# The MLP of a decoder trunk: one level of Strassen's scheme in its expanding product, and eight chunks of hidden channels for four

## The chip, the cores and the metric

One core of one Trainium2 chip. Times are device microseconds of one execution, and a kernel's time is the median of its runs. TensorE (PE) multiplies, VectorE (DVE), ScalarE (ACT) and GpSimd (POOL) do the rest, SyncE (SP) starts transfers.

## The reference

Two layers on 512 tokens of 1024 channels, all float32. What matters here is the second half of a layer, with 4096 hidden channels:

```python
u = rms_norm(h, mlp_norm_w[l])
h = h + jnp.square(jax.nn.relu(u @ w_mlp_in[l])) @ w_mlp_out[l]
```

The first half (three token mixers from one input product, and an output product into the residual stream) and the final norm stay as they are.

## The kernel before

The residual stream lies channel-major in SBUF: eight tiles `h[m]` of 128 channels by 512 tokens. Every dense product is exact to nearly float32 by splitting each operand into two float32r parts, high and low. A k tile then takes three matmuls, high by high, high by low and low by high, added up in PSUM. `load_w` (L875) fetches a tile of weights, 128 x 4 x 256, as `raw`; a copy (ACT or DVE) makes its high part `whi`, and a subtraction `raw - whi` its low part `wlo`. The norm's factor for each token is applied after the expanding product (it commutes with relu): `finish_h` (L809) squares a finished `h[m]` into the sum `sqa`, and splits `h[m]` times the norm's weight into `u`; `norm_stats` makes the row of factors `rb`.

The MLP (L1102) goes through the hidden channels in 4 chunks of 1024: `expand(q)` (8 tiles of 128 channels by 512 tokens, 24 matmuls of 512 columns each, `mm_cm`), then relu times `rb`, the square, and its split into `hh` and `hl`; `contract(q)` adds the chunk's share to the eight `h[m]`. The order in the program is expand(0), expand(1), contract(0), and so on. The last chunk of the last layer contracts token-major, with 256 columns (`mm_tm`), since the final norm goes on from there.

Nothing runs in program order. A recorder takes down every operation (in the profile all have L483, pairs of attention products L1275). A list scheduler then fixes one order per engine from the costs in `cost` (matmul: columns/2.4 + 2.7 ns; GpSimd: 80 + 2.2 ns a column), with 12 rounds of forward and backward schedules, and each engine runs its list strictly in order. An operation that several engines could do (`copy`: ACT or DVE; `tt`: DVE or GpSimd) goes to its first choice unless another would be done clearly earlier. How many tiles of a kind exist is set by `CAPS` (L523): a tile's slot is reused when its last reader is done. The costs know of no influence of one engine on another.

Of the kernel before, what the change touches and what calls it, by code (L numbers as in the profile page):

```python
# [10 lines left out]
F32 = mybir.dt.float32  # L11
# [56 lines left out]
class Buf:  # L68
    """A tile, allocated when its first instruction is emitted."""
# [26 lines left out]
class View:  # L96
    """A part of a tile: the steps that lead to it, and its shape."""
# [85 lines left out]
class Recorder:  # L183
    """Records the instructions, orders them for the engines, and emits them in that order."""
# [38 lines left out]
    def add(self, eng, run, outs, ins, dur, lat=0.0):  # L223
# [9 lines left out]
        # a product's start clears its whole bank  # L233
# [17 lines left out]
    def order(self):  # L251
        """List schedules: first by the longest path, then by the start times of a backward schedule."""
# [28 lines left out]
    def backward(self, span):  # L281
        """From the end, with the tiles in the order they had: the latest starts."""
# [34 lines left out]
    def forward(self):  # L317
# [37 lines left out]
        while done < len(ops):  # L355
# [25 lines left out]
            # the tiles it allocates  # L381
# [20 lines left out]
            if op.ways:  # L402
                # the first way's engine has it unless another would be done with it clearly earlier
# [60 lines left out]
class _Engine:  # L464
# [23 lines left out]
    def cost(self, method, named, views):  # L488
# [6 lines left out]
        if self.eng == "PE":  # L495
# [8 lines left out]
            return (112.0 if m <= 64 else 214.0), 0.0  # L504
# [18 lines left out]
CAPS = {"u": 16, "un": 28, "hw": 6, "lg": 10, "pt": 4, "raw": 2, "whi": 4, "wlo": 4, "t2": 5, "mm": 3, "mx": 5, "hq": 4,  # L523
# [6 lines left out]
class Build:  # L530
# [10 lines left out]
    def tile(self, shape, dt=F32, tag=None):  # L541
        """A tile of a tag's slots; without a tag, one that stays."""
# [38 lines left out]
    # ---------------------------------------------------------------- setup  # L581
    def setup(self):
# [3 lines left out]
        # the tensor engine at its full clock before the input is there  # L586
# [10 lines left out]
        # the input, channel-major  # L597
# [210 lines left out]
    # ---------------------------------------------------------------- norms  # L808
    def finish_h(self, m, key, l, src=None):  # L809
        """h[m] is final: its squares, and its split and weighted form for the next products."""  # L810
# [4 lines left out]
        if key is not None:  # L815
# [30 lines left out]
    def row_bc(self, cols, o=None):  # L846
        """cols [128 tokens of a tile, 4 tiles] -> [128, 512], each row the 512 tokens' values."""
# [52 lines left out]
    def load_cols(self, pieces, n, per):  # L900
        """pieces: (column in the tile, DRAM AP [1024, columns]) -> split weights, per rows of 128 to a tile."""
# [14 lines left out]
    def mm_cm(self, out, w, c0, m, x, kts=range(KT)):  # L916
        """channel-major: out[m channels, 512 tokens]."""
# [9 lines left out]
    def mm_tm(self, out, t, w, n, x):  # L927
        """token-major: out[128 tokens of tile t, n columns]."""
# [8 lines left out]
    # ---------------------------------------------------------------- one layer  # L937
    def layer(self, l):
# [7 lines left out]
        # --- the indexer's queries; latent keys; the values of the sparse attention with the indexer's keys and weights  # L946
# [28 lines left out]
        # --- small weights of the layer  # L975
# [15 lines left out]
        # the second part's halves, one under the other  # L991
# [4 lines left out]
        # --- latent queries  # L996
# [23 lines left out]
        # --- gated linear recurrence, two heads at a time  # L1020
# [29 lines left out]
        # --- sparse attention  # L1050
# [30 lines left out]
        # --- output product  # L1081
# [20 lines left out]
        # --- MLP  # L1102
        self.norm_stats()
        x, rb = self.u, self.rb
        hid = [None] * 4

        def expand(q):
            tags = ["un"] * 16 if q % 2 == 0 else ["un"] * 2 + ["lg"] * 8 + ["hw"] * 6
            H = [self.tile((128, 512), F32R, t) for t in tags]
            H = (H[:8], H[8:])  # L1110
            for j in range(4):
                c = q * 1024 + j * 256
                w = self.load_w([(0, a["w_mlp_in"][l][:, c:c + 256])], 256, False)
                for i in range(2):
                    m = 2 * j + i
                    p = self.psm()
                    self.mm_cm(p, w, i * 128, 128, x)
                    r, r2 = self.t2(), self.t2()
                    hh, hl = H[0][m], H[1][m]
                    nc.vector.scalar_tensor_tensor(r, p, 0.0, rb, op0=OP.max, op1=OP.mult)  # L1120
                    nc.square(hh, r)
                    nc.tt(r2, r, r, OP.mult)
                    nc.tt(hl, r2, hh.bitcast(F32), OP.subtract)
            hid[q] = H
# [63 lines left out]
    def index_scores(self, l, qi, ki, wi):  # L1188
        """0 for the selected keys and -NEG for the others, for the query tiles that have more than N_SEL keys."""
# [45 lines left out]
                # float32r is at its full rate from 256 columns on  # L1235
# [30 lines left out]
    def pair(self, po, vals, PT, k):  # L1266
        """Two heads' products, side by side on the array."""
# [89 lines left out]
    # ---------------------------------------------------------------- gated linear recurrence  # L1357
# [12 lines left out]
    def hgrn_head(self, l, hd, hf, pq, vi, gate, cq, mix):  # L1370
# [82 lines left out]
        # the norm over the head's channels, the gate  # L1453
# [104 lines left out]
```

## Time and profile before

| | |
|---|---|
| median of three runs | 1389.15 us (1389.15 to 1390.95) |
| profiled execution: time of the runs beside it / its span | 1389.15 / 1388.4 us |
| PE busy | 1349.8 us, 97% |
| DVE, ACT, POOL busy | 903.3, 546.9, 175.3 us |
| mean granted TensorE clock over the span | 0.989 |
| moved by DMA | 131.52 MB, mean 95 GB/s |

A busy share is an average over parts of the program that differ. A wait counts if the engine that waits is the one that the end of the program hangs on; so the stretches, the chain that ended last and the idle time before single instructions are read along with it.

### The profile page before, as it was taken

How to read it: one execution, taken by the hardware profiler on the slowest of the kernel's cores; microseconds unless marked ns; L12 is line 12 of the kernel's file. 1: busy time of each engine (PE TensorE's matmuls, PEld its weight loads, DVE VectorE, ACT ScalarE, POOL GpSimd, SP SyncE). 2: the span in 40 equal slices, each digit the busy share in tenths (PEclk: the TensorE clock that was granted, in tenths of full speed). 3: DMA queues.
4: the chain of work that ended last, by engine and by line, in shares of the span. 5: the costliest groups of instructions: out<-in, count | busy, mean ns of one | idle time of the engine just before them, and what ended most of it. 6: DMA issues, size and time to landing. Idle time of an engine off the chain costs nothing.

```text
span 1388.4 us, 17965 instructions
## 1 busy us (share of the span) xinstructions
PE 1349.8 (97%) x6693; PEld 1094.5 (79%) x6693; DVE 903.3 (65%) x1863; ACT 546.9 (39%) x1002; POOL 175.3 (13%) x145
## 2 busy tenths in 40 slices
PE   8899999999999999999999999999999999999998
PEld 5688887767788878878778878877678888878897
DVE  6979999795755354354446999988586534534444
ACT  5556447364333122132234674546343312312233
POOL 3213223040100000000002213214010000000000
PEclk9999999999999999999999999999999999999999
DMA  7433121143233333232435212223332323233322
GB/s 229 119 109 88 46 77 47 53 146 124 73 101 95 93 102 96 83 99 91 136 106 120 62 31 76 76 69 102 118 92 81 113 79 106 91 91 107 104 80 76
DMA packets 137083, 131.52 MB, mean 95 GB/s; under 512 B 14068, under 2 KB 129540, under 8 KB 136996
## 3 DMA queue, kind: packets, MB, share of 16 engines
q1 hardware_dynamic: 135716, 127.62, 30.5%
q0 software_dynamic: 1280, 2.77, 0.9%
q8 instruction: 52, 0.85, 0.3%
q14 instruction: 35, 0.29, 0.1%
HBM read 121.44 MB, written 8.92 MB: 94 GB/s over the span
## 4 chain that ended last, share of the span: by engine, by line
PE 83%; DVE 12%; issue 2%; ACT 2%; DMA 1%; SPq 0%; DVEq 0%; ACTq 0%
PE mm L483 73%; PE mx L483 9%; DVE un L483 5%; DVE c L483 2%; DVE t L483 1%; DVE lg L483 1%; PE mx L1275 1%; DVE wlo L483 1%; DVE hw L483 1%; DMA raw<-in_w_in_dram 1%; ACT t L483 1%; ACT un L483 0%; DVE sqa L483 0%; DVE ge L483 0%; ACT whi L483 0%
## 5 line engine op out<-in xcount | busy, mean ns | idle before, releaser
L483 PE MATMUL mm<-u,whi 128*128 128x512 f32 x1632 | 515.0, 403 | 5.4 <-ACT whi L483 3.6
L483 ACT ACTIVATE whi<-raw 128x1024 fp32r<-128x1024 f32 (+2 forms) x198 | 205.3, 1039 | 480.7 <-PE mm L483 437.5
L483 PEld LDWEIGHTS mm<-u,whi 128*128 128x128 f32 x1632 | 305.5, 189 | 78.1 <-ACT whi L483 4.2
L483 DVE TENSOR_TENSOR wlo<-raw,whi 128x1024 fp32r<-128x1024 f32 (+1 forms) x170 | 207.9, 1225 | 219.0 <-ACT whi L483 183.8
L483 PE MATMUL mm<-u,wlo 128*128 128x512 f32 x816 | 293.9, 401 | 2.5 <-DVE wlo L483 2.5
L483 PE MATMUL mm<-un,whi 128*128 128x512 f32 x816 | 260.1, 401 | 3.2 <-DVE un L483 3.1
L483 PEld LDWEIGHTS mm<-un,whi 128*128 128x128 f32 x816 | 153.5, 189 | 41.7 <-DVE un L483 3.7
L483 PEld LDWEIGHTS mm<-u,wlo 128*128 128x128 f32 x816 | 153.2, 188 | 39.2 <-DVE wlo L483 3.3
L483 PE MATMUL mm<-un,wlo 128*128 128x512 f32 x432 | 159.4, 400 | 0.0
L483 DVE TENSOR_TENSOR un<-mm,un 128x512 f32<-128x512 f32 (+2 forms) x120 | 77.6, 652 | 118.0 <-PE mm L483 106.8
L483 PE MATMUL mm<-whi,u 128*128 128x256 f32 (+1 forms) x640 | 139.5, 304 | 0.4 <-DVE un L483 0.3
L483 POOL TENSOR_TENSOR wlo<-raw,whi 128x1024 fp32r<-128x1024 f32 (+3 forms) x38 | 92.1, 2424 | 311.6 <-ACT whi L483 204.7
L483 PE MATMUL mx<-un,un 128*128 128x512 f32 (+3 forms) x380 | 117.0, 374 | 10.0 <-DVE un L483 7.2
L483 PEld LDWEIGHTS mm<-whi,u 128*128 128x128 f32 x640 | 103.8, 192 | 10.5 <-issue 6.2
L483 PEld LDWEIGHTS mm<-un,wlo 128*128 128x128 f32 x432 | 81.7, 190 | 19.4 <-issue 0.7
L483 PEld LDWEIGHTS mx<-un,un 128*128 128x128 f32 x380 | 69.2, 195 | 25.6 <-DVE un L483 9.1
L483 DVE SCALAR_TENSOR_TENSOR t<-mm,rb 128x512 f32<-128x512 f32 x68 | 46.6, 689 | 64.7 <-PE mm L483 63.6
L483 PE MATMUL mm<-wlo,u 128*128 128x256 f32 (+1 forms) x320 | 84.9, 306 | 0.0
L483 PE MATMUL mm<-lg,whi 128*128 128x512 f32 x192 | 70.3, 395 | 0.0
L483 ACT ACTIVATE un<-t 128x512 fp32r<-128x512 f32 (+1 forms) x63 | 39.6, 630 | 64.1 <-DVE t L483 62.3
L483 PEld LDWEIGHTS mm<-wlo,u 128*128 128x128 f32 x320 | 56.8, 192 | 3.3 <-issue 2.1
L483 PE MATMUL mm<-hw,whi 128*128 128x512 f32 x144 | 54.7, 394 | 0.0
(203 smaller groups left out, 1664.6 us busy)
## 6 DMA issues: line engine op xcount, KB each, us to landing
raw<-in_w_mlp_in_dram SPq DMA_DIRECT2D x64, 512.0 KB, 3.6
raw<-in_w_mlp_out_dram SPq DMA_DIRECT2D x64, 512.0 KB, 3.5
raw<-in_w_in_dram SPq DMA_DIRECT2D x42, 512.0 KB, 3.8
d<-un SPq DMA_DIRECT2D x20, 256.0 KB, 3.2
raw<-in_w_in_dram SPq DMA_DIRECT2D x18, 256.0 KB, 3.2
raw<-in_w_out_dram SPq DMA_DIRECT2D x16, 256.0 KB, 2.7
raw<-in_w_out_dram SPq DMA_DIRECT2D x8, 512.0 KB, 3.4
un<-d SPq DMA_DIRECT2D x16, 256.0 KB, 4.9
```

Source lines behind the costliest of these rows:

```text
L483: real(*[res(v) for v in args], **{k: res(v) for k, v in kw.items()})
L1275: self.real.tensor.matmul(outs[i].get(), vals[i].get(), rhs[i].get(), start=k == 0, stop=k == NT - 1)
```

## The change

With the input x and a weight matrix of one chunk cut into quarters (by 512 channels in, and 256 tokens or 256 hidden channels), the expanding product needs eight products of quarters. The changed kernel takes seven, in the Strassen-Winograd form: products of sums and differences of quarters, whose results are added up. A chunk is now 512 hidden channels, and there are eight. The sums over x (`forms`) are made once per layer, the differences of weights in each chunk. Matmuls have 256 columns (half the tokens). The contraction stays a plain product, also cut into 256 columns. The caps and the costs of PE change with it. Comments and docstrings are gone, which says nothing.

```diff
-                return n * (1 if n >= 256 else 4) / 2.4 + 2.7, 0.0
+                return n * (0.4453 if n >= 256 else 1.7) + 4.0, 0.0
-CAPS = {"u": 16, "un": 28, ... "pt": 4, "raw": 2, "whi": 4, "wlo": 4, "t2": 5, ...
+CAPS = {"u": 16, "un": 24, ... "pt": 3, "raw": 5, "whi": 5, "wlo": 5, "t2": 6, ...
+        if key == "mn":
+            self.forms(m, self.v(key, l, m))
+    def forms(self, m, w):
...
+        f = self.un()
+        nc.copy(f, hm, w)
+        if m < 4:
+            hi, lo = self.X["X11"][k]
+            nc.copy(hi, f[:, half[0]])
+            nc.tt(lo, f[:, half[0]], hi.bitcast(F32), OP.subtract)
+            return
+        nc.copy(hi, f)
+        nc.tt(lo, f, hi.bitcast(F32), OP.subtract)
+        nc.tt(S1, x21, x22, OP.add)
+        nc.tt(S3, x11, x21, OP.subtract, True)
+        nc.tt(S2, S1, x11, OP.subtract)
+        nc.tt(S4, x12, S2, OP.subtract)
+        if k % 2:
+            for n, t in self.S.items():
+                nc.copy(hi, t)
+                nc.tt(lo, t, hi.bitcast(F32), OP.subtract)
...
+        def activate(q, c, i, b):
+            nc.vector.scalar_tensor_tensor(v(r), v(c), 0.0, tok, op0=OP.max, op1=OP.mult)
+            nc.square(hh, r)
+            nc.tt(r, r, r, OP.mult, True)
+            nc.tt(hl, r, hh.bitcast(F32), OP.subtract)
         def expand(q):
+            A, B, C = self.ps(), self.psm(), self.ps()
+            s11 = split(w11)
+            nc.tt(w11, w12, w11, OP.subtract, True)
+            product(A, "X11", s11, True, False)
+            p1 = self.t2()
+            nc.copy(p1, A)
+            product(B, "X12", split(w21), True, True)
+            nc.vector.tensor_tensor(out=p1, in0=B, in1=p1, op=OP.add)
+            activate(q, p1, 0, 0)
+            nc.tt(w12, w22, w12, OP.subtract, True)
+            s22 = split(w22)
+            nc.tt(w22, w22, w11, OP.subtract, True)
+            product(A, "S2", split(w22), False, False)
+            u = self.t2()
+            nc.copy(u, A)
+            product(C, "S1", split(w11), True, False)
+            p5 = self.t2()
+            nc.copy(p5, C)
+            product(A, "S3", split(w12), False, False)
+            nc.vector.tensor_tensor(out=p5, in0=A, in1=p5, op=OP.add)
+            activate(q, p5, 1, 1)
+            product(C, "S4", s22, False, True)
+            nc.vector.tensor_tensor(out=u, in0=C, in1=u, op=OP.add)
+            activate(q, u, 0, 1)
+            nc.tt(w21, w21, w22, OP.subtract, True)
+            product(A, "X22", split(w21), False, True)
+            activate(q, A, 1, 0)
         def contract(q):
...
+                    for i in range(2):
+                        o = p[:, i * 256:i * 256 + 256]
+                        for k in range(4):
+                            xh, xl = (x(i, k, part) for part in range(2))
+                            nc.tensor.matmul(o, wh[:, k, ms], xh, start=k == 0, stop=False)
+                            nc.tensor.matmul(o, wh[:, k, ms], xl, start=False, stop=False)
+                            nc.tensor.matmul(o, wl[:, k, ms], xh, start=False, stop=k == 3)
```

`split` makes a high and a low part of a tile of weights, `product` runs 2 x 4 x 3 matmuls into one PSUM bank, and `True` as the last argument of `nc.tt` names GpSimd as first choice. The differences of weights are written over the raw tiles in place.

What this does to the order is shown at the start of an MLP's product and in a steady chunk. First DVE in a steady chunk before (names: a kind of tile, the tile's number, the number of the operation that wrote it; out<-in); `raw`, `whi`, `wlo` are weights, `t2` and `un` hidden channels, `mm` a PSUM bank:

```order
L483 TENSOR_TENSOR wlo_1081_4137<-raw_1079_4069,whi_1080_4130 128x1024
L483 SCALAR_TENSOR_TENSOR t2_1046_4156<-mm_1045_4034,rb_993_3993 128x512
L483 TENSOR_TENSOR t2_1047_4164<-t2_1046_4156 128x512
L483 TENSOR_TENSOR un_1011_4170<-t2_1047_4164,un_1003_4162 128x512
L483 SCALAR_TENSOR_TENSOR t2_1049_4177<-mm_1048_4089,rb_993_3993 128x512
L483 TENSOR_TENSOR wlo_1084_4182<-raw_1082_4117,whi_1083_4173 128x1024
```

One subtraction of weights stands to about three operations on hidden channels. DVE in chunk 4 of layer 0 now, where `un<-mm,un` are additions into the residual stream and `raw_1219` to `raw_1222` the four quarters of weights w11, w12, w22 and w21:

```order
L483 TENSOR_TENSOR wlo_1227_5532<-raw_1219_5328,whi_1226_5455 128x1024
L483 TENSOR_TENSOR un_919_3522<-mm_1203_5451,un_919_3522 128x512
L483 TENSOR_TENSOR un_927_3678<-mm_1207_5475,un_927_3678 128x512
L483 TENSOR_TENSOR un_929_3680<-mm_1208_5490,un_929_3680 128x512
L483 TENSOR_TENSOR wlo_1230_5567<-raw_1222_5425,whi_1229_5528 128x1024
L483 TENSOR_TENSOR wlo_1234_5580<-raw_1221_5402,whi_1233_5556 128x1024
L483 SCALAR_TENSOR_TENSOR t2_1196_5593<-mx_1170_4993,rb_1021_4138 128x512
L483 TENSOR_TENSOR raw_1221_5402<-raw_1221_5402,raw_1219_5328 128x1024
L483 TENSOR_TENSOR raw_1222_5425<-raw_1222_5425,raw_1221_5402 128x1024
L483 TENSOR_TENSOR un_1198_5633<-t2_1196_5593,un_1197_5602 128x512
L483 TENSOR_TENSOR wlo_1236_5640<-raw_1221_5402,whi_1235_5622 128x1024
```

Four subtractions for splits and two of the differences of weights stand there among the additions. GpSimd beside it now:

```order
L483 TENSOR_TENSOR raw_1219_5328<-raw_1220_5356,raw_1219_5328 128x1024
L483 TENSOR_TENSOR raw_1220_5356<-raw_1221_5402,raw_1220_5356 128x1024
L483 TENSOR_TENSOR t2_1196_5593<-t2_1196_5593 128x512
L483 TENSOR_TENSOR t2_1228_5614<-t2_1228_5614 128x512
```

The other two differences and the squares are GpSimd's. On PE the last use of `wlo_1201`, whose slot `wlo_1227` takes, is the first row here, and the first uses of the difference w22 - w11' (`whi_1235`, `wlo_1236`, for the product with S2 into the bank `mx_1223`) are the third and the last; 84 and 93 matmuls lie between:

```order
L483 MATMUL mm_1203_5451<-un_1137_4945,wlo_1201_5343 128x256
...
L483 MATMUL mm_1213_5586<-un_1145_5156,whi_1210_5392 128x256
L483 MATMUL mx_1223_5469<-hw_965_3937,whi_1235_5622 128x256
L483 MATMUL mm_1212_5562<-un_1144_5125,wlo_1211_5408 128x256
...
L483 MATMUL mm_1212_5562<-un_1138_4980,whi_1210_5392 128x256
L483 MATMUL mx_1223_5469<-hw_965_3937,wlo_1236_5640 128x256
```

PE takes the matmuls of the contraction (`mm`) and of the products (`mx`) in turn. At the start of the MLP of layer 0, DVE before had additions into the residual stream, the sum of squares and the low parts `u`:

```order
L483 TENSOR_TENSOR sqa_959_3759<-sqa_959_3759,t2_987_3881 128x512
L483 SCALAR_TENSOR_TENSOR u_978_3909<-un_939_3515,k_26_151,u_977_3899 128x512
L483 SCALAR_TENSOR_TENSOR u_982_3918<-un_947_3713,k_26_151,u_981_3911 128x512
L483 SCALAR_TENSOR_TENSOR u_986_3926<-un_949_3724,k_26_151,u_985_3920 128x512
```

GpSimd had the last subtractions of `load_w` for the output product there. Now it has four differences of weights, sums over x and squares (DVE has as many sums over x beside these, and the splits):

```order
L483 TENSOR_TENSOR raw_1027_3310<-raw_1028_3574,raw_1027_3310 128x1024
L483 TENSOR_TENSOR raw_1028_3574<-raw_1029_3620,raw_1028_3574 128x1024
L483 TENSOR_TENSOR u_960_3827<-un_983_3810,u_958_3821 128x256
L483 TENSOR_TENSOR raw_1029_3620<-raw_1029_3620,raw_1027_3310 128x1024
L483 TENSOR_TENSOR un_992_3865<-un_977_3771,un_989_3851 128x256
L483 TENSOR_TENSOR raw_1030_3669<-raw_1030_3669,raw_1029_3620 128x1024
L483 TENSOR_TENSOR un_993_3900<-un_992_3865,un_977_3771 128x256
```

Of the seven rows four write over raw weights, and three make sums over x that go into the forms.

## Rows read from the trace of the kernel before

**Rows 1.** Page, part 1: busy us, share of the span, instructions by engine.

```profile
PE 1349.8 (97%) x6693; PEld 1094.5 (79%) x6693; DVE 903.3 (65%) x1863; ACT 546.9 (39%) x1002; POOL 175.3 (13%) x145
```

**Rows 2.** Stretches inside the MLPs: PE, PEld, DVE, ACT, POOL, clock, DMA share, GB/s.

```profile
380.00:520.00 140.00, 139.79 (x603) 112.84 (x602) 69.06 (x84) 37.53 (x43) 1.86 (x1) 1.00 0.31 95
1040.00:1320.00 280.00, 280.00 (x1206) 225.84 (x1206) 131.62 (x158) 70.14 (x79) 5.63 (x5) 1.00 0.32 98
```

**Rows 3.** Chain that ended last, MLP steps: start, us, engine, tile, count.

```profile
364.46 152.09 PE mm L483 x655
...
1032.79 288.27 PE mm L483 x1240
...
1343.67 29.33 PE mm L483 x248
```

**Rows 4.** Groups by form, 360 to 760: busy, mean ns; idle before, releaser.

```profile
L483 DVE TENSOR_TENSOR wlo<-raw,whi 128x1024 fp32r<-128x1024 f32 x68 | 83.2, 1223 | 118.1 <-ACT whi L483 92.0 <-PE mm L483 26.1
L483 ACT ACTIVATE whi<-raw 128x1024 fp32r<-128x1024 f32 x68 | 72.1, 1061 | 212.7 <-PE mm L483 181.6 <-DVE t L483 11.8 <-issue 10.2
L483 DVE TENSOR_TENSOR un<-mm,un 128x512 f32<-128x512 f32 x32 | 22.1, 690 | 45.6 <-PE mm L483 45.5
```

**Rows 5.** Groups by form of GpSimd, whole span.

```profile
L483 POOL TENSOR_TENSOR wlo<-raw,whi 128x1024 fp32r<-128x1024 f32 x32 | 78.0, 2436 | 268.6 <-ACT whi L483 192.3 <-PE mm L483 66.7 <-DVE whi L483 4.8
...
L483 POOL TENSOR_TENSOR sqa<-sqa,t 128x512 f32<-128x512 f32 x3 | 3.9, 1284 | 266.3 <-ACT t L483 263.6 <-ACT sqa L483 2.3 <-DVE t L483 0.5
...
L483 POOL TENSOR_TENSOR hw<-hw,c 128x256 f32<-128x256 f32 x4 | 2.6, 648 | 7.1 <-DVE hw L483 7.1
```

**Rows 6.** Timeline of GpSimd, 335 to 360: start, us, instruction, idle before.

```profile
342.87 2.41 POOL L483 TENSOR_TENSOR wlo<-raw,whi 128x1024 fp32r<-128x1024 f32 x1 [31.70 <-ACT whi L483]
349.99 2.97 POOL L483 TENSOR_TENSOR wlo<-raw,whi 128x1024 fp32r<-128x1024 f32 x1 [4.71 <-ACT whi L483]
```

**Rows 7.** Timeline of DVE, the same time.

```profile
341.77 1.22 DVE L483 TENSOR_TENSOR wlo<-raw,whi 128x1024 fp32r<-128x1024 f32 x1
342.90 0.68 DVE L483 TENSOR_TENSOR un<-mm,un 128x512 f32<-128x512 f32 x1
343.50 2.33 DVE L483 TENSOR_TENSOR sqa<-sqa,t 128x512 f32<-128x512 f32 x1
345.76 0.68 DVE L483 TENSOR_TENSOR un<-mm,un 128x512 f32<-128x512 f32 x1
...
350.02 0.68 DVE L483 TENSOR_TENSOR sqa<-sqa,t 128x512 f32<-128x512 f32 x1
350.62 2.90 DVE L483 SCALAR_TENSOR_TENSOR u<-un,k,u 128x512 fp32r<-128x512 f32 x1
```

**Rows 8.** Timeline of PE at the start of the MLP of layer 0.

```profile
346.49 1.20 PE L483 MATMUL mm<-un,whi 128*128 128x512 f32 x4 [1.21 <-DVE un L483]
...
355.43 0.44 PE L483 MATMUL mx<-k,sqa 128*128 128x64 f32 x2 [1.36 <-DVE sqa L483]
```

**Rows 9.** Stretches where PE pauses, columns as in rows 2.

```profile
350.00:360.00 10.00, 8.64 (x42) 6.82 (x41) 8.72 (x17) 4.87 (x9) 2.96 (x1) 1.00 0.18 52
970.00:975.00 5.00, 2.98 (x16) 2.20 (x15) 4.71 (x9) 1.78 (x8) 3.60 (x2) 1.00 0.86 300
975.00:980.00 5.00, 4.76 (x21) 3.01 (x22) 4.85 (x16) 2.89 (x7) 0.04 (x1) 0.66 0.36 112
```

**Rows 10.** Timeline of DVE near the end.

```profile
1373.02 0.76 DVE L483 TENSOR_TENSOR un<-mm,un 128x256 f32<-128x256 f32 x2 [3.94 <-PE mm L483]
...
1381.74 0.42 DVE L483 TENSOR_TENSOR un<-mm,un 128x256 f32<-128x256 f32 x1
```

**Rows 11.** Timeline of PE, its last matmul.

```profile
1381.36 0.27 PE L483 MATMUL mm<-whi,hw 128*128 128x256 f32 x1
```

**Rows 12.** Timeline of SP's queue, the transfers of the output.

```profile
1376.35 9.05 SPq L483 DMA_DIRECT2D out_dram<-t  x8
```

**Rows 13.** Page, part 6: loads of the expanding weights, KB each, us to landing.

```profile
raw<-in_w_mlp_in_dram SPq DMA_DIRECT2D x64, 512.0 KB, 3.6
```

More of the change, by code (lines that the diff above doesn't have):

```diff
@@ L520, in cost @@
         return 68.0 + n / 0.96, 0.0
-CAPS = {"u": 16, "un": 28, "hw": 6, "lg": 10, "pt": 4, "raw": 2, "whi": 4, "wlo": 4, "t2": 5, "mm": 3, "mx": 5, "hq": 4,
+CAPS = {"u": 16, "un": 24, "hw": 6, "lg": 10, "pt": 3, "raw": 5, "whi": 5, "wlo": 5, "t2": 6, "mm": 3, "mx": 5, "hq": 4,
         "hS": 3, "ge": 1, "sqa": 1, "rb": 1, "c1": 20, "c4": 24, "c8": 8, "c16": 4, "bst": 1, "bmv": 1, "wi": 1}
@@ L814, in finish_h @@
             nc.sync.dma_start(self.hd[m], hm)
-        if key is not None:
+        if key == "mn":
+            self.forms(m, self.v(key, l, m))
+        elif key is not None:
             if m == 0:
@@ L831, in finish_h @@
             nc.tt(self.sq_acc, self.sq_acc, sq, OP.add)
+    def forms(self, m, w):
+        nc = self.nc
+        half = (slice(0, 256), slice(256, 512))
+        if m == 0:
+            self.uf, self.X, self.S = [], {}, {}
+            extra = ["lg"] * 8 + ["hw"] * 4
+            for n, name in enumerate(("X11", "X22", "S1", "S2", "S3", "S4")):
+                if name == "X22":
+                    continue
+                tags = [extra.pop() if n > 2 and extra else "u" for _ in range(4)]
+                t = [self.tile((128, 2, 256), F32R, tag) for tag in tags]
+                self.X[name] = [(t[k // 2][:, k % 2, :], t[2 + k // 2][:, k % 2, :]) for k in range(4)]
+                self.X[name, "t"] = t
+            self.X["X12"], self.X["X22"] = [], []
+        hm, k = self.h[m], m % 4
+        f = self.un()
+        self.uf.append(f)
+        nc.copy(f, hm, w)
[4 more added lines that the diff above has]
+            return
+        hi, lo = (self.tile((128, 512), F32R, "u") for _ in range(2))
+        nc.copy(hi, f)
+        nc.tt(lo, f, hi.bitcast(F32), OP.subtract)
+        for i, name in enumerate(("X12", "X22")):
+            self.X[name].append((hi[:, half[i]], lo[:, half[i]]))
+        x11, x21, x12, x22 = (self.uf[n][:, half[i]] for n, i in ((k, 0), (k, 1), (m, 0), (m, 1)))
+        if k % 2 == 0:
+            self.S = {n: self.un(F32, (128, 2, 256)) for n in ("S1", "S2", "S3", "S4")}
+        S1, S2, S3, S4 = (self.S[n][:, k % 2, :] for n in ("S1", "S2", "S3", "S4"))
+        nc.tt(S1, x21, x22, OP.add)
[4 more added lines that the diff above has]
+            for n, t in self.S.items():
+                hi, lo = self.X[n, "t"][k // 2], self.X[n, "t"][2 + k // 2]
+                nc.copy(hi, t)
+                nc.tt(lo, t, hi.bitcast(F32), OP.subtract)
     def rsqrt_cols(self, x, n=4):
@@ L1103, in layer @@
         self.norm_stats()
-        x, rb = self.u, self.rb
-        hid = [None] * 4
-        def expand(q):
[L1108 to L1124, printed above, removed]
+        rb = self.rb
@@ new lines, in layer, with split, product @@
+        hid = {}
+        def split(t):
+            hi, lo = self.tile((128, 4, 256), F32R, "whi"), self.tile((128, 4, 256), F32R, "wlo")
+            nc.copy(hi, t)
+            nc.tt(lo, t, hi.bitcast(F32), OP.subtract)
+            return hi, lo
+        def product(out, name, w, start, stop):
+            for m in range(2):
+                o = out[:, m * 256:m * 256 + 256]
+                for k in range(4):
+                    xh, xl = self.X[name][k]
+                    ws = [x[:, k, m * 128:m * 128 + 128] for x in w]
+                    nc.tensor.matmul(o, ws[0], xh, start=start and m == 0 and k == 0, stop=False,
+                                     skip_group_check=True)
+                    nc.tensor.matmul(o, ws[0], xl, start=False, stop=False, skip_group_check=True)
+                    nc.tensor.matmul(o, ws[1], xh, start=False, stop=stop and k == 3, skip_group_check=True)
@@ new lines, in expand @@
+        def expand(q):
+            W = a["w_mlp_in"][l]
+            raw = {}
+            for k, b in ((0, 0), (0, 1), (1, 1), (1, 0)):
+                t = raw[k, b] = self.tile((128, 4, 256), F32, "raw")
+                c = q * 512 + b * 256
+                nc.sync.dma_start(t, W[k * 512:k * 512 + 512, c:c + 256].rearrange("(k p) n -> p k n", p=128))
+            w11, w12, w22, w21 = raw[0, 0], raw[0, 1], raw[1, 1], raw[1, 0]
+            A, B, C = self.ps(), self.psm(), self.ps()
[25 more added lines that the diff above has]
+            activate(q, A, 1, 0)
@@ L1126, in contract @@
         def contract(q):
-            last = q == 3 and l + 1 == DEPTH
+            last = q == 7 and l + 1 == DEPTH
             if last:
                 self.turn()
+            x = lambda i, k, part: hid[q, i, k // 2][part][:, k % 2 * 256:k % 2 * 256 + 256]
             for j in range(4):
-                w = self.load_w([(0, a["w_mlp_out"][l][q * 1024:(q + 1) * 1024, 256 * j:256 * j + 256])], 256, False)
+                t = self.tile((128, 4, 256), F32, "raw")
+                W = a["w_mlp_out"][l][q * 512:q * 512 + 512, 256 * j:256 * j + 256]
+                nc.sync.dma_start(t, W.rearrange("(k p) n -> p k n", p=128))
+                wh, wl = split(t)
@@ L1135, in contract @@
                         first = len(nc.ops)
-                        self.mm_tm(p[:, 0:256], t, w, 256, hid[q])
+                        ts = slice(t % 2 * 128, t % 2 * 128 + 128)
+                        for k in range(4):
+                            xh, xl = (x(t // 2, k, part)[:, ts] for part in range(2))
+                            nc.tensor.matmul(p[:, 0:256], xh, wh[:, k, :], start=k == 0, stop=False)
+                            nc.tensor.matmul(p[:, 0:256], xh, wl[:, k, :], start=False, stop=False)
+                            nc.tensor.matmul(p[:, 0:256], xl, wh[:, k, :], start=False, stop=k == 3)
                         if t:
```

22 lines of the change are left out of this document (14 added, 8 removed).

## The prediction

> **What bounds the kernel now.** I read the busy shares first, then the stretches, the chain, the groups of lines, and last single instructions. The reader is to see in the first that TensorE (PE) is busy for 97% of the span [rows 1]; 1388.4 - 1349.8 = 38.6 us is all that waits can cost today. In the stretches: inside both MLPs PE has no idle time, with VectorE (DVE) at about a half, and the granted clock is 1.00, the 2.4 GHz level [rows 2]. In the chain: the MLP is one unbroken run of matmuls [rows 3]. Hence an MLP is worth its number of matmuls times the duration of one, until something else becomes late. From the first and third entry of [rows 3], 152.09/655 = 0.2322 us for a matmul of 512 columns and 29.33/248 = 0.1183 us for one of 256, each with its own weight load.
>
> **Term 1, matmuls.** Before, an MLP expands with 32 column tiles x 24 matmuls and contracts with 4 x 8 x 24, all of 512 columns, but for the very last part of layer 1, which has 4 x 4 x 24 = 384 of 256 columns in place of 192 of 512. So both layers have 2 x 1536 - 192 = 2880 of 512. After, a chunk expands with 7 products x 2 x 4 x 3 = 168 and contracts with 8 x 2 x 4 x 3 = 192, all of 256 columns: 16 x 360 = 5760, 5376 more than the 384. Cost: -2880 x 0.2322 + 5376 x 0.1183 = -668.7 + 635.8 = **-32.9 us**. Of it the product left out, 384 narrow matmuls, is -45.4, and cutting 2880 wide ones in two gives 12.7 back (2 x 0.1183 against 0.2322). The Trainium skill speaks against this step: "TensorE: Matmul & The Clock Gate", section "Back-to-back issue gap", has about 81 ns for a run of 128 columns and 131 ns at 512, about 98 at 256 as an estimate between them; 5376 x 98 - 2880 x 131 ns would be a loss of 149 us. The rows of this kernel's own f32r matmuls stand at 232 and 118 ns, nearly in the ratio of the columns, so the trace doesn't agree and decides.
>
> **Term 2, what else is added, and the lock.** Per chunk come 4 sums of weights of 1024 columns, 7 splits (a copy, mostly on ACT, and a subtraction) where the products needed 4, copies out of PSUM, and twice as many additions into the residual stream: in all DVE gets 48 subtractions of 1024, 64 additions and 48 scaled maxima of 512, GpSimd 44 sums of 1024 and 32 squares of 512. DVE is idle for half of an MLP [rows 2], so in amount it fits: 48 x 1.22 [rows 4] + 112 x 0.69 + some 60 for the rest is about 200 us, against about 300 us idle. In latency it need not. A tensor_tensor of 1024 columns on GpSimd took 2.41 us [rows 5, 6], and while it ran, from 342.87 to 345.28, the addition of DVE that reads PSUM took its 0.68 us, but the next, with both inputs in SBUF, 2.33 us in place of 0.68 [rows 7]. At 349.99 it was the other way about: GpSimd's took 2.97, about 0.56 more than 2.41, beside a DVE one from 350.02 to 350.62, and then DVE's lasted 2.90. So two such instructions go one after the other. "SBUF — State Buffer", section "Who interferes with whom", in the Trainium skill says the same, that the lock of the shared port pair is held for the whole instruction, and that an instruction with one SBUF input doesn't take part; by it every pair of such instructions is serial, which the trace's few pairs bear out. The order was made without it: it lays GpSimd's sums beside DVE's splits.
>
> **Term 3, waits in a steady chunk.** I walked chunk 4 of layer 0 by hand, with the spacing that DVE shows back to back [rows 7]: 341.77 to 342.90 is 1.13 for 1024 columns, 342.90 to 343.50 is 0.60 for 512; ACT's copy is 1.06 [rows 4]. The clock starts when PE's last use of wlo_1201 frees that slot for wlo_1227. From there to the first use of wlo_1236 PE has 93 matmuls, 11.0 us; whi_1235 is due after 84, 9.9 us. DVE: wlo_1227 0.4 to 1.5, three additions from PSUM to 3.3; GpSimd may write the difference over raw_1219 at 1.7 and ends at 4.1; only then the subtractions wlo_1230 and wlo_1234, to 6.4; the maximum from PSUM to 7.0, beside GpSimd's next sum, 6.4 to 8.8; the sums raw_1221 and raw_1222 to 11.2; ACT copies whi_1235 by 11.2; GpSimd's square 1.28 [rows 5] to 12.5; then un_1198 and wlo_1236, 14.3, and a hop of 0.1. PE is held 1.3 us at whi_1235 and 2.1 more at wlo_1236: 3.4 us. In the same walk without the lock wlo_1236 is done at 10.3 and nothing waits. Matmuls of the next groups are queued behind the held one, and they free the next slots later, so nothing is caught up on PE.
> Of the 14 chunks after each layer's first, five of layer 0 (3 to 7) have this shape: 17.0 us. The others differ; in layer 1 PE has 161 matmuls, 19.0 us, against a walk of 19.7: I take 0.7 for each of seven, 4.9, and nothing for the last two. A pause also lowers the clock: after about 2 us of PE idle in 970 to 975 the next 5 us were granted 0.66, between the two levels, 1.7 us lost; after 1.36 us in 350 to 360 it stayed at 1.00 [rows 8, 9]. Half of 1.7 at five pauses is about 4. **+26**. Bounds: below, 0 if the engines run ahead and the lock only eats slack; above, 14 x (3.4 + 1.7) = 71.
>
> **Term 4, the start of an MLP.** Between the last residual tiles and the products, `forms` now makes five sets of splits. From the end of tile 0's last output product to the first use of the last forms PE has 42 x 0.2322 + 110 x 0.1183 = 22.8 us of work; over that GpSimd has four sums of 1024 (2.44), ten of 256 (0.65) and six of 512 (1.28) [rows 5], 23.9 us, and DVE four of 1.13, fourteen of 0.60, and thirteen of about 0.34 (0.42 for one alone [rows 10], less the 0.08 that the others lose back to back), 17.3. All serial that is 41.2, so PE would idle 18.4, where today it idles 1.21 + 1.36 = 2.57 [rows 8]. The lower end is about 2.6 + 2 idle: both engines overlap wherever an input is in PSUM or the other waits for ACT. I take the middle between +2 and +16 for each layer: **+18** (0 to +32).
>
> **Term 5, the rest.** The last matmul group ends at 1381.63 and the span 6.8 us later [rows 11, 12]. A tile of the last part has 12 matmuls now, 1.42 us, in place of 24; DVE stood idle for 3.94 us before the additions of a tile [rows 10], so the vector work of the last tiles bunches: +2 (1 to 4). Loads: 64 of 512 KB for each weight matrix as now, 3.6 us each [rows 13], DMA at a third [rows 2], five raw slots for two: nothing, and 0.3 us a wait if that cover went. Attention is reordered by the new slots (24 for 28, 3 for 4) and new costs: 0, bounded by a quarter of the 38.6 idle, -10 to +10.
>
> **Sum.** -32.9 + 26 + 18 + 2 = +13.1 on 1388.4, 1401.5; around the span the measured time has 1389.15 - 1388.4 = 0.75 (the median of the three runs, which the profiled execution matches). **1402.**
>
> **Rivals.**
> First, the waits are absorbed: DVE, half idle, and GpSimd run a chunk ahead because five slots of raw, whi and wlo allow it, and the lock takes slack only. For it: 200 us of work in 300; against it: slots, not work, set the start of my walk. Then -32.9 + 2 for the end, and from 0 to +15 at the starts and elsewhere: 1358 to 1386, likeliest 1368.
> Second, and the worse side: the lock is fully serial at both starts and in every chunk, as queues can't reorder. It decides if a chunk's walk is later than PE's work by over 2 us also in layer 1. Then -32.9 + 14 x 3.4 + 2 x 15.8 + 2 + half of 14 x 1.7 is +60, 1449; with some chunks clear, 1418 to 1440.
> Third, that the product doesn't shrink: the counts rule it out. Narrow matmuls costing more than 0.1183 would need 0.1244 to eat the gain; 248 in a row say otherwise.
>
> **Numbers.** My case, 1392 to 1418: 0.45. The first rival, 1358 to 1386: 0.38. The second, above 1418: 0.11. Between the first two, 1386 to 1392: 0.06; within 0.2% (2.8 us, about what a measurement can tell from no change) as much. Faster 0.38, slower 0.56. A range of 1364 to 1430 leaves out about 0.08 at each end, the upper part of the bounds among them.
>
> **What would show it.** In the profile after: matmuls of 256 columns at 0.118 back to back; PE's busy time down by about 33; PE idle before groups whose second input is whi or wlo, released by DVE, 2 to 4 us in chunks 3 to 7 of layer 0; GpSimd's sums at 2.4 to 3.5 us; DVE subtractions of 2 to 3.5 us beside them; 5 to 14 us of PE idle at the start of each MLP. Wrong it is if PE stays at 1.00 busy through the MLPs (the first rival), or if the matmuls run slower than 0.1183.

## The result, and the profile after

| | before | changed |
|---|---|---|
| median | 1389.15 us (1389.1 to 1390.95, 4 runs) | 1493.45 us (1489.57 to 1497.19, 4 runs) |
| ratio | | 1.0752, 95% interval 1.0729 to 1.0776 |
| profiled execution: time / span | 1389.15 / 1388.4 us | 1495.73 / 1494.0 us |
| mean granted clock | 0.989 | 0.965 |

Slower, as forecast, but by 104 us where 13 were forecast, and outside the range. First the busy shares and the end of the chain of the changed kernel; they answer to [rows 1, 3].

```profile
PE 1362.0 (91%) x9189; PEld 1222.8 (82%) x9189; DVE 1161.1 (78%) x2079; ACT 602.8 (40%) x1080; POOL 375.4 (25%) x251
```

```profile
1469.28 10.24 PE mm L483 x87
```

87 matmuls in 10.24 us are 0.1177 us each, so the price of a matmul was right. But PE is idle for 1494.0 - 1362.0 = 132.0 us, where it was 38.6. Its busy time rose by 12.2 although the matmuls should need 32.9 less: the clock has to answer for about (1 - 0.965) x 1494.0 = 52 us against 15, 37 more; some 8 us I can't divide. Where it stands, by stretches, columns as in [rows 2]: the mixers of layer 0, the end of the output product, the start of the MLP's products, the rest of the MLP; then the same of layer 1 (whose MLP is one row before). The cut between output product and MLP is the first matmul of the norm between them. First before:

```profile
28.05:320.00 291.95, 278.90 (x1546) 226.80 (x1545) 258.30 (x688) 158.68 (x349) 73.06 (x58) 0.98 0.31 87
320.00:355.43 35.43, 32.86 (x143) 24.89 (x142) 26.32 (x32) 16.31 (x23) 5.39 (x2) 1.00 0.36 113
355.43:380.00 24.57, 24.57 (x110) 20.06 (x111) 14.46 (x31) 7.30 (x11) 1.95 (x1) 1.00 0.24 73
380.00:730.00 350.00, 349.30 (x1504) 281.40 (x1502) 162.82 (x197) 94.68 (x110) 5.56 (x3) 1.00 0.33 99
730.00:985.00 255.00, 246.76 (x1408) 200.68 (x1408) 223.07 (x600) 138.01 (x314) 69.27 (x57) 0.99 0.29 81
985.00:1023.70 38.70, 36.31 (x158) 27.14 (x156) 26.68 (x32) 16.90 (x27) 5.04 (x2) 1.00 0.28 85
1023.70:1367.00 343.30, 343.30 (x1627) 283.69 (x1627) 164.62 (x222) 91.67 (x122) 5.63 (x5) 1.00 0.30 94
```

and after:

```profile
30.35:345.00 314.65, 292.72 (x1576) 237.52 (x1577) 262.44 (x704) 153.61 (x342) 64.98 (x57) 0.96 0.30 88
345.00:382.41 37.41, 25.78 (x122) 20.22 (x120) 32.16 (x35) 19.52 (x30) 25.33 (x15) 0.94 0.14 43
382.41:420.00 37.59, 30.36 (x206) 28.67 (x207) 34.19 (x43) 12.31 (x18) 20.58 (x11) 0.88 0.13 41
420.00:794.00 374.00, 345.53 (x2745) 336.81 (x2745) 265.50 (x274) 111.78 (x134) 93.68 (x54) 0.98 0.34 101
794.00:1060.00 266.00, 252.85 (x1423) 204.06 (x1422) 223.60 (x605) 139.12 (x313) 53.20 (x44) 0.99 0.24 70
1060.00:1107.00 47.00, 34.55 (x150) 26.68 (x148) 34.03 (x40) 21.93 (x36) 22.76 (x13) 0.91 0.21 68
1107.00:1145.00 38.00, 31.86 (x218) 29.95 (x219) 34.96 (x47) 13.74 (x21) 18.69 (x10) 0.89 0.23 70
1145.00:1479.50 334.50, 321.95 (x2640) 319.82 (x2640) 244.70 (x275) 107.23 (x139) 64.22 (x33) 0.97 0.28 86
```

Length less PE's busy time is its idle time; one less the clock, times the length, is about what the clock took (it has two digits here, so to some 2 us in a long stretch). The second and third stretch of a layer I call its start, the fourth its steady part. So counted, the two starts have 37.4 us of idle time where they had 5.0, and lost 15 us to the clock where they lost nothing; the steady parts 41.0 where they had 0.7, and 17.5 where they lost nothing; the mixers with the 30 us ahead of the first norm 43.4 where they had 26.1, and 17 where they lost 12. What PE waited for in the two steady parts (us in total, times, longest), 420.00 to 794.00:

```profile
PE mm L483 <- DVE un L483: 10.9, 9, 1.8
PE mx L483 <- DVE wlo L483: 8.9, 6, 2.1
PE mx L483 <- ACT whi L483: 5.3, 4, 1.4
PE mx L483 <- DVE whi L483: 1.8, 1, 1.8
...
```

and 1145.00 to 1479.50:

```profile
PE mm L483 <- DVE un L483: 9.0, 4, 3.2
PE mx L483 <- DVE wlo L483: 2.6, 2, 1.8
PE mx L483 <- ACT whi L483: 0.9, 1, 0.9
```

Half of it, 19.9 us, is at matmuls of the contraction (`mm`). What such waits are, PE's rows in chunks 4 (the one walked, up to 550.00) and 5 of layer 0 show; columns as in [rows 8]:

```profile
547.38 0.39 PE L483 MATMUL mx<-hw,whi 128*128 128x256 f32 x1 [1.25 <-ACT whi L483]
550.00 0.38 PE L483 MATMUL mx<-hw,wlo 128*128 128x256 f32 x1 [1.30 <-DVE wlo L483]
...
580.64 0.75 PE L483 MATMUL mm<-un,whi 128*128 128x256 f32 x4 [1.78 <-DVE un L483]
590.14 0.39 PE L483 MATMUL mm<-un,whi 128*128 128x256 f32 x1 [1.20 <-DVE un L483]
596.61 0.39 PE L483 MATMUL mx<-hw,whi 128*128 128x256 f32 x1 [1.37 <-ACT whi L483]
600.00 0.58 PE L483 MATMUL mx<-hw,wlo 128*128 128x256 f32 x1 [2.07 <-DVE wlo L483]
```

DVE and GpSimd in chunk 5:

```profile
575.46 0.69 DVE L483 CAST whi<-raw 128x1024 fp32r<-128x1024 f32 x1 [1.05 <-PE mm L483]
...
576.67 3.31 DVE L483 TENSOR_TENSOR wlo<-raw,whi 128x1024 fp32r<-128x1024 f32 x1
579.91 0.68 DVE L483 TENSOR_TENSOR un<-mm,un 128x512 f32<-128x512 f32 x1
...
585.27 2.89 DVE L483 CAST whi<-raw 128x1024 fp32r<-128x1024 f32 x1
...
596.06 2.75 DVE L483 TENSOR_TENSOR un<-t,un 128x512 fp32r<-128x512 f32 x1
598.73 1.21 DVE L483 TENSOR_TENSOR wlo<-raw,whi 128x1024 fp32r<-128x1024 f32 x1
```

```profile
576.50 2.39 POOL L483 TENSOR_TENSOR wlo<-raw,whi 128x1024 fp32r<-128x1024 f32 x1 [4.67 <-ACT whi L483]
582.39 5.22 POOL L483 TENSOR_TENSOR raw<-raw,raw 128x1024 f32<-128x1024 f32 x2 [3.50 <-DVE wlo L483]
593.08 5.18 POOL L483 TENSOR_TENSOR raw<-raw,raw 128x1024 f32<-128x1024 f32 x2 [5.47 <-issue]
```

The walk had 1.3 and 2.1 us at `whi` and `wlo`: it is 1.25 and 1.30 in chunk 4, 1.37 and 2.07 in chunk 5. But before these stand, in chunk 5, 1.78 and 1.20 at matmuls of the contraction, which the walk had not: the addition that empties the bank (579.91) takes its 0.68 us, but it is queued behind a subtraction that stood from 576.67 to 579.91 while GpSimd ran. So it is at all eleven waits of over 0.5 us for such an addition in the two steady parts: in the 7 us before each, a DVE instruction takes longer than its own time beside GpSimd. A locked instruction holds up what is behind it, not itself alone.

### The profile page after: what moved, and what is told of

Its sections match the earlier page's. It is cut to its first block, busy times and chain, and to the rows that moved or that the text cites. A ratio compares the mean times of both kernels' runs of the same rounds, so it can differ in the third digit from the quotient of the medians.

```text
span 1494.0 us, 23406 instructions
## 1 busy us (share of the span) xinstructions
PE 1362.0 (91%) x9189; PEld 1222.8 (82%) x9189; DVE 1161.1 (78%) x2079; ACT 602.8 (40%) x1080; POOL 375.4 (25%) x251
## 5 line engine op out<-in xcount | busy, mean ns | idle before, releaser
L483 PE MATMUL mm<-un,whi 128*128 128x256 f32 (+1 forms) x2176 | 463.5, 302 | 33.4 <-DVE un L483 33.3
L483 ACT ACTIVATE whi<-raw 128x1024 fp32r<-128x1024 f32 (+3 forms) x234 | 243.7, 1043 | 499.6 <-PE mm L483 278.5
L483 PEld LDWEIGHTS mm<-un,whi 128*128 128x128 f32 x2176 | 354.9, 193 | 52.6 <-DVE un L483 35.8
L483 DVE TENSOR_TENSOR wlo<-raw,whi 128x1024 fp32r<-128x1024 f32 (+2 forms) x222 | 288.2, 1304 | 86.6 <-ACT whi L483 58.0
L483 PE MATMUL mm<-u,whi 128*128 128x512 f32 (+1 forms) x864 | 278.0, 379 | 15.4 <-DVE u L483 5.8
L483 PE MATMUL mm<-un,wlo 128*128 128x256 f32 (+1 forms) x1088 | 278.3, 300 | 0.0
L483 PE MATMUL mx<-u,whi 128*128 128x256 f32 x768 | 202.5, 287 | 6.4 <-DVE t L483 4.6
L483 PEld LDWEIGHTS mm<-u,whi 128*128 128x128 f32 x864 | 164.2, 193 | 45.2 <-DVE u L483 7.1
L483 PEld LDWEIGHTS mx<-u,whi 128*128 128x128 f32 x768 | 146.8, 193 | 8.3 <-DVE t L483 5.0
L483 PE MATMUL mm<-u,wlo 128*128 128x512 f32 (+1 forms) x432 | 150.9, 375 | 0.0
```

Source lines behind the costliest of these rows:

```text
L483: real(*[res(v) for v in args], **{k: res(v) for k, v in kw.items()})
```

## The experiments

Each was timed against the kernel before on the same chip (whose median was 1388.0 to 1389.0 us each time); times are medians, ratios are to the kernel before with their 95% interval. "Mixers" is the time from the first norm's first matmul to the second's in layer 0, 327.4 us before and 352.1 in the changed kernel.

**Is it GpSimd in the MLP?** `vt` is a tensor_tensor on DVE alone; one line of several is shown.

```diff
# in forms, split, activate, expand
-nc.tt(lo, t, hi.bitcast(F32), OP.subtract)
+nc.vt(lo, t, hi.bitcast(F32), OP.subtract)
```

> The changed kernel with every tensor_tensor of the MLP and of the sums over x on DVE; GpSimd has nothing left there. Theory 1 (the MLP's waits come from the serial lock between DVE and GpSimd, and from queueing behind locked instructions): the PE idle of the steady chunks, 28.5 us in layer 0 and 12.6 in layer 1, falls below 10 in all, the clock loss there with it, and the two starts get shorter by 10 to 15 us each although DVE has more to do (11.5 us at its own speed for 23.9 at GpSimd's): 1410 to 1430. Theory 2 (the waits come from the amount and the queue of DVE work itself, GpSimd or not): DVE's busy share rises, PE idle stays, 1470 to 1510.

1404.08 us, 1.0102 (1.0085 to 1.0119): theory 1, and below its range; 89 us of the 104 come back. PE's idle time at the two starts falls from 37.4 to 16.3 us. The steady part in layer 0 and in layer 1:

```profile
411.00:741.58 330.58, 329.62 (x2692) 324.67 (x2691) 253.91 (x312) 105.73 (x126) 17.98 (x13) 1.00 0.37 109
1082.80:1392.00 309.20, 308.77 (x2600) 308.13 (x2601) 237.41 (x312) 97.60 (x131) 2.94 (x3) 1.00 0.29 90
```

DVE does all the work of 64 activations and 64 differences, is busy for 77%, and PE waits for 1.4 us in 640, at full clock.

Whether it was the lock, or only that a slow GpSimd instruction stood in the chain, the next one tells: work on GpSimd that stands in no chain.

```diff
 # e1_no_pool_mlp, in activate
+g, x = self.tile((128, 256), F32, "ge"), hl.bitcast(F32)
+for _ in range(4):
+    nc.gpsimd.tensor_tensor(out=g, in0=x[:, 0:256], in1=x[:, 256:512], op=OP.mult)
```

> e1_no_pool_mlp, plus work on GpSimd whose result nobody reads: four products of 256 columns behind each of the 64 activations (4 x 0.65 us, about 10 us in a chunk, as much as GpSimd had there in the changed kernel). It leaves out nothing. If the lock makes the waits: DVE's busy time in the MLPs rises by 40 us or more, PE's idle time in the steady chunks comes back from 1.5 to over 15 us, and 1430 to 1480. If it was that GpSimd's slower instructions stood in the chain of the weights: the work is in no chain, so 1398 to 1410.

1442.26 us, 1.0389 (1.0358 to 1.0421), 38 more than e1. The same stretches:

```profile
410.40:764.70 354.30, 337.67 (x2687) 329.16 (x2688) 279.86 (x314) 106.25 (x127) 159.47 (x137) 0.99 0.35 103
1100.60:1428.00 327.40, 314.18 (x2589) 311.28 (x2588) 258.80 (x308) 98.09 (x132) 144.85 (x132) 0.98 0.28 85
```

Idle time is back, 16.6 and 13.2 us, and DVE is busy for 47 us more with the same work. (GpSimd is busy for 304 us in these two stretches, where it was 158 in the changed kernel, so the run shows the cause and not its size there.) DVE's groups over the whole span, in the changed kernel, in e1 and in e9, tell the lock from mere slowness:

```profile
L483 DVE TENSOR_TENSOR un<-mm,un 128x512 f32<-128x512 f32 x152 | 102.2, 685 | 76.7 <-PE mm L483 70.2 <-DMA un<-d 5.8
L483 DVE TENSOR_TENSOR un<-t,un 128x512 fp32r<-128x512 f32 x56 | 62.3, 1112 | 7.9 <-POOL t L483 6.9
```

```profile
L486 DVE TENSOR_TENSOR un<-mm,un 128x512 f32<-128x512 f32 x152 | 101.8, 683 | 50.6 <-PE mm L486 47.8 <-DMA un<-d 2.6
L486 DVE TENSOR_TENSOR un<-t,un 128x512 fp32r<-128x512 f32 x64 | 43.6, 686 | 1.1
```

```profile
L486 DVE TENSOR_TENSOR un<-mm,un 128x512 f32<-128x512 f32 x152 | 102.0, 682 | 43.4 <-PE mm L486 40.9 <-DMA un<-d 2.1
L486 DVE TENSOR_TENSOR un<-t,un 128x512 fp32r<-128x512 f32 x64 | 55.5, 871 | 1.5
```

With one input in PSUM 0.68 us in all three; with both in SBUF 0.686 where GpSimd is quiet, 1.112 and 0.871 where it isn't. That is what the Trainium skill has in "SBUF — State Buffer", section "Who interferes with whom".

Part of GpSimd's work taken away (the four differences of weights):

```diff
-nc.tt(w11, w12, w11, OP.subtract, True)   # and w12, w22, w21
+nc.vt(w11, w12, w11, OP.subtract)
```

> The changed kernel with only the four differences of weights of a chunk on DVE; GpSimd keeps the squares, some splits and its sums over x. By the lock, GpSimd's busy time in the MLPs (about 200 us over those of e1) falls by half, and the loss against e1_no_pool_mlp (90 us) to about a third: 1425 to 1445. If only the differences, being the longest, matter: 1402 to 1412. If they don't: 1475 to 1495.

1433.85 us, 1.0326 (1.0307 to 1.0345): of what the changed kernel loses against e1 a third is left, with GpSimd busy for 306 us in place of 375, so it isn't the differences alone.

**Does it need GpSimd gone, or an order that knows the lock?** The planner of the next one gives DVE and GpSimd one port:

```diff
+# tensor_tensor, scalar_tensor_tensor, tensor_copy, tensor_scalar of DVE, POOL without PSUM: lock
+            s = t
+            if getattr(op.run, "lock", False):
+                s = max(t, port)
+                port = s + op.dur
-            free[e] = t + op.dur
-            op.end = t + op.dur + op.lat
+            free[e] = s + op.dur
+            op.end = s + op.dur + op.lat
```

(In this and the kernels that build on it, and in e12, ties between slots are broken by a tile's number.)

> The changed kernel with the planner of e14_plain_first_lock_known, its own costs and slots, GpSimd still first choice for the differences. If the planner's ignorance of the lock was the cause: it gives most of the loss back, 1400 to 1430. If a GpSimd instruction of 2.4 us that shuts out DVE costs whatever the order: 1450 to 1490.

1417.6 us, 1.0206 (1.0185 to 1.0227): 76 us come back though GpSimd is busy for 466 us, where it was 375 in the changed kernel. Nearly all of it lies in the MLPs: from one norm to the next, or to the end, these take 368.6 and 358.8 us in place of 411.7 and 387.1. The steady part of layer 0 waits for 1.3 us, that of layer 1 for 3.6; the start of layer 0 still for 9.5 + 4.4 at clocks of 0.87 and 0.86:

```profile
336.40:373.42 37.02, 27.54 (x128) 21.60 (x127) 36.45 (x36) 21.56 (x36) 33.61 (x23) 0.87 0.10 29
373.42:411.40 37.98, 33.63 (x236) 32.37 (x237) 32.15 (x43) 15.87 (x22) 15.60 (x8) 0.86 0.36 111
411.40:742.04 330.64, 329.34 (x2685) 323.78 (x2684) 249.15 (x254) 113.54 (x135) 103.69 (x56) 1.00 0.36 106
1100.10:1407.00 306.90, 303.29 (x2544) 301.23 (x2543) 228.88 (x253) 98.73 (x133) 89.67 (x46) 1.00 0.28 87
```

So in the steady parts it was the order: the lock costs a steady chunk next to nothing where the order leaves room for it, though DVE's instructions stand as long as before (`un<-t,un` has a mean of 1.032 us, for 1.112). At the starts the order gives little back, 31.9 us of 37.4 are left. (The rule for ties came with the rule of the port here; apart they were run only from e12 to e14 below.)

**Why did the mixers, whose code is the same, get longer?** The costs alone, in the kernel before:

```diff
-return n * (1 if n >= 256 else 4) / 2.4 + 2.7, 0.0
+return n * (0.4453 if n >= 256 else 1.7) + 4.0, 0.0
-return (112.0 if m <= 64 else 214.0), 0.0
+return (130.0 if m <= 64 else 214.0), 0.0
```

> The kernel before with only the PE costs of the changed one (0.4453 n + 4.0, 1.7 n + 4, 130). The token mixers became 20 to 25 us longer in the changed kernel. If the new costs made the worse order there: 1405 to 1415, with the stretches 28 to 320 and 730 to 985 longer by 8 to 12 us each. If it was the slots (24 un for 28, 3 pt for 4): 1386 to 1392.

1418.45 us, 1.0208 (1.0193 to 1.0223), mixers 344.1. That is over the 1405 to 1415 expected: the costs that fit the matmuls best (0.232 and 0.118 us) made the old kernel 29 us slower. Only the second line of the two:

> The kernel before with only the cost of a small plain-float32 matmul at 130 ns for 112. If that part made e2_before_new_costs slow: 1412 to 1420. If it was the 7% on the large matmuls: 1386 to 1392. If any change of the costs throws the order of the mixers into another, no better or worse one: anything from 1385 to 1420, not tied to which cost it was.

1391.66 us, 1.0016 (1.0005 to 1.0027), mixers 327.8: so by elimination it was the first line, 7% on the matmuls of 512 columns, unless the two lines do it only together. Whether such a cost makes a worse order, or any change of costs only another one, is not shown. The other way about, the old costs in the changed kernel and in e1:

> The changed kernel with the PE costs of the kernel before, GpSimd as it was. If the costs and GpSimd's share in the MLP are two causes that add up: 1494 - 25 = 1460 to 1475, with the PE idle of the MLPs unchanged at 75 us or so. If the costs that fit the chip help the MLP's order: over 1490.

1471.39 us, 1.0596 (1.058 to 1.0612), mixers 341.9, 10 shorter than in the changed kernel. But the MLPs changed too: PE's idle time in them is 56 us and not the 75 expected.

> e1_no_pool_mlp with the PE costs of the kernel before. If the new costs make the order of the token mixers worse also here, as e2_before_new_costs showed in the old kernel (+29): 1370 to 1385, faster than both, with the mixers' stretches at about 291 and 254 to 258 us. If the slots (24 un, 3 pt) rule there now: 1398 to 1408.

1395.23 us, 1.0048 (1.0031 to 1.0065), mixers 332.0; a miss, as 1370 to 1385 was expected. The two causes add up only roughly: 22 us come from the costs with GpSimd, 9 without. The slots, with new costs and with old:

```diff
-CAPS = {... "un": 24, "pt": 3, "raw": 5, "whi": 5, "wlo": 5, ...
+CAPS = {... "un": 28, "pt": 4, "raw": 4, "whi": 4, "wlo": 4, ...
```

> As e1_no_pool_mlp, and the slots un 28 and pt 4 as in the kernel before, paid with raw 4, whi 4, wlo 4 in place of 5. If the slots made the token mixers longer: 10 to 20 us below e1_no_pool_mlp, unless fewer weight slots give waits in the MLP. If not: the same as e1 within 4 us, or slower by the waits for raw, whi and wlo.

> e5_slots_back with the PE costs of the kernel before. If e5_slots_back was slow by an unlucky order of the mixers and not by the slots: 1375 to 1395. If fewer weight slots cost as such: about 1395 + 18 = 1413.

1422.38 us, 1.0243 (1.0227 to 1.0258), and 1401.83, 1.0103 (1.0082 to 1.0125), the latter between the two values expected. More slots for the mixers, paid with slots for weights, made both slower than e1 and e6. The mixers, 347.2 and 333.0, are no shorter than in e1 (342.9) and e6 (332.0), so these two don't show the slots as what made them long. The last test is the planner with the lock, in the kernel before:

> The kernel before with the planner of e14_plain_first_lock_known. If ignoring the lock costs there too: 1365 to 1382. If its order was fitted or lucky: 1385 to 1400.

1386.93 us, 0.998 (0.9966 to 0.9994): hardly faster, and not the 1365 to 1382 that were to show a cost of ignoring the lock there. Mixers are 316.9 in the profiled execution, 10 below those before, but that was the fastest of ten (1380.61).

**Is it the chunks, and what do narrow matmuls and the starts cost?** The kernel before in eight chunks:

```diff
-c = q * 1024 + j * 256      # for j in range(4), 4 chunks
+c = q * 512 + j * 256       # for j in range(2), 8 chunks; contract over 4 k tiles
```

> The kernel before with the MLP in 8 chunks of 512 hidden channels, plain products and matmuls of 512 columns. If the number of matmuls and nothing of the chunks counts in a steady MLP: 1385 to 1393, PE idle inside the MLPs under 2 us. If smaller chunks cost by themselves (twice the additions into the residual stream): 1395 to 1410.

1393.66 us, 1.0039 (1.0026 to 1.0052): just over the first range, 5 us more than before, and its PE waits for under 2 us in its MLPs. So smaller chunks cost a plain MLP next to nothing. Hidden tiles by all tokens, on e6:

```diff
-hh, hl = self.uns(2, F32R)          # 2 x 128 channels, 256 tokens
+hh, hl = (x[:, i * 256:i * 256 + 256] for x in hid[q, 2 * b + e])
-o = p[:, i * 256:i * 256 + 256]     # 24 matmuls of 256 columns
+nc.tensor.matmul(p, wh[:, k, ms], xh, start=k == 0, stop=False)   # 12 of 512
```

> e6_no_pool_old_costs with hidden tiles of 128 channels by all 512 tokens (two squares and two subtractions of 256 columns behind each activation in place of one of 512), so that the contraction runs with matmuls of 512 columns, 12 for 24. By 24 x 0.1183 - 12 x 0.2322 = 0.053 us for each of 2 x 8 x 8 tiles, less the last part: 6.4 us less, 1389. If narrow matmuls cost nothing over wide ones: 1395. The order of the mixers, which is remade, may move either by 5 to 10.

1422.99 us, 1.0248 (1.0228 to 1.0268): inconclusive. The order of the mixers was remade at 360.5 us, 28 more than in e6, and hides the 6 expected. Then, on e11, the first chunk plain:

```diff
 def expand(q):
+    if q == 0:
+        return plain(q)     # 4 x 24 matmuls of 512 columns, as in the kernel before
```

> e11_wide_contraction with the first chunk of each MLP by plain products of 512 columns, so that the sums over x are wanted a chunk later, and slots u 20, raw 4, wlo 4 for it. If the two starts are what e6_no_pool_old_costs still loses (PE idle of 17.9 us around them against 5.0 before, and the clock after it): 10 to 18 us less than e11 after 4.8 us for the added matmuls, 1372 to 1382. If it is the order of the mixers: 1388 to 1400.

1391.34 us, 1.0017 (1.0006 to 1.0028), mixers 333.1: a miss for the starts, as 1372 to 1382 was expected. PE's idle time at the starts fell from 22.9 us in e11 to 12.6; most of the 32 us gained is the order of the mixers, 27 shorter than in e11. And the same kernel with the planner that knows the lock, the only difference:

> e12_plain_first_chunk with a planner that knows the lock: an instruction on DVE or GpSimd that reads only SBUF starts no sooner than the last such one on either has ended. If the mixers (PE idle 17 and 13 us, the clock after it) are long because their order ignores the lock: 1365 to 1382, faster than both. If their length is chance of the order: anything from 1375 to 1405. If the slots (un 24, pt 3) make it: 1388 to 1394.

1378.04 us, 0.9927 (0.9905 to 0.9948): 13 us less than e12, faster than both kernels, and 9 less than the kernel before with the same planner (e15). Mixers, 322.5 us, with 24 un and 3 pt. Its busy shares, then the start and the rest of the MLP of layer 0:

```profile
PE 1325.9 (96%) x7605; PEld 1118.4 (81%) x7605; DVE 1111.3 (81%) x2165; ACT 614.4 (45%) x1151; POOL 214.8 (16%) x174
```

```profile
320.00:357.10 37.10, 34.05 (x133) 26.33 (x134) 25.01 (x32) 17.65 (x26) 6.73 (x3) 0.91 0.41 134
357.10:395.00 37.90, 36.30 (x221) 31.33 (x220) 36.51 (x68) 19.54 (x29) 6.29 (x1) 1.00 0.19 59
395.00:717.94 322.94, 321.51 (x1888) 281.99 (x1887) 245.30 (x315) 115.20 (x162) 18.26 (x12) 1.00 0.35 105
```

PE waits for 4.7 us at this start, where the changed kernel's waited for 18.9, and for 1.4 in the rest. It is the saving of the product with its waits nearly gone: PE is busy for 1325.9 us against 1349.8. Of these 24 us 10 are lost again, as over the whole span PE is idle for 48.6 against 38.6.

## Why the prediction was right or wrong

The forecast was +13.1 us, the profiled spans differ by 105.6. Of the 92 between them term 3 misses 32, term 4 29, term 5 22, the tail 1, and some 8 stay undivided.

- **Term 1, -32.9: right.** 0.1177 us a narrow matmul; and where the waits are gone the busy time falls by 23 us (e6), with a clock of 0.983 for 0.989 still in it, 8 us.
- **Term 2, the lock: right** for tensor_tensors, shown by e9.
- **Term 3, +26: the walk was right, what it left out failed**: 40.3 us of idle time and 17.5 of clock. In the five chunks of layer 0 that the walk stood for, the pair of waits was 2.56, 2.55, 3.44, 3.45 and 3.57 us, 15.6 in all for 17.0; in layer 1 such waits were 3.5 for 4.9. What the term put at nothing is the queue: 19.9 us at matmuls of the contraction. I took the additions from PSUM as free of the lock because they don't take part in it, and didn't ask what stands ahead of them. And I priced the clock at five pauses, 4 us; in 1145 to 1479.5 alone, 12.6 us of idle time came with a clock of 0.97, 10 us.
- **Term 4, +18: too small**, 32.4 of idle time, and 15 of clock, which the term had left out. The idle time is the upper bound of the sum: the two engines one after the other gave 18.4 us for a start, and 18.9 and 18.6 were measured. Between bounds far apart I took the middle without a row for it. That the match is so close is in part luck: with GpSimd out (e1) 16.3 of the 37.4 us stay, with an order that knows the lock (e16) 31.9, so the lock alone doesn't make it.
- **Term 5, 0 for the mixers: failed, +17 of idle time and 5 of clock**, over the bound of 10. A changed cost of PE reorders everything, the parts whose code is the same too. e2 has 29 us from that alone. The bound had been a share of today's idle time, which is no bound on an order made anew. The tail, +2, measured 14.50 us from 1479.5, with PE idle for 10.1 there, against 6.8: +3.
- The rivals: the second (serial at both starts and in all chunks, 1418 to 1440, with all of it 1449) was nearest, and too low by what the mixers, the queue and the clock took. The first, that the waits are absorbed, was wrong for this order; the steady parts of e16 show it once the order allows it.
- That it is slower at all doesn't bear out terms 3 and 4 by itself: e1, with the steady waits gone, is slower by 15 us too, through its mixers (342.9) and starts.

What stays open: why one order of the mixers is 10 or 40 us longer than another. With 24 un and 3 pt they took 322.5 to 360.5 us, with 28 and 4 316.9 to 347.2, so slots alone don't decide; the order that knows the lock was the shortest in e14 and e15, each of its group, but not in e16 (334.4).

## What to carry to other kernels

Work moved to GpSimd isn't free because GpSimd is idle: while its tensor_tensors ran here, DVE instructions that read only SBUF stood, and all that was queued behind them, the additions that empty PSUM banks among them. Put it beside PSUM reads, tell the scheduler of it, or leave it on DVE, which did the same in half the time (1.2 us for 2.4 at 1024 columns). And where one list scheduler orders the whole program, price a change of its costs as a change of every part, with a run of that change alone.

## What the runs showed of the hardware

A cast on DVE with one SBUF input also stood still beside GpSimd: 2.89 us at 585.27 for 0.69 at 575.46. So what term 2 says of an instruction with one SBUF input holds for the tensor_tensors that read PSUM beside it (0.68 us), and not for this cast.

Short pauses can lose clock: 12.6 us of waits, none longer than 3.2, came with 0.97 in layer 1's steady part, while 1.4 us of waits in 640 (e1) left it at 1.00. Their sum doesn't decide it: the steady part of layer 0 in e7 kept 1.00 with 14.6 us of waits, none longer than 1.7.

```profile
410.00:764.45 354.45, 339.85 (x2741) 331.57 (x2741) 262.02 (x279) 113.75 (x135) 81.92 (x42) 1.00 0.35 105
```
